# Score matmuls of two attentions with queries stacked high over low, and a reordered attention stage

## The chip, the cores and the metric

The kernel runs on one core of one Trainium2 chip. The metric is the device time in microseconds of one execution. The engines that matter are TensorE (PE; its weight loads are shown apart as PEld), VectorE (DVE), ScalarE (ACT), GpSimd (POOL) and SyncE (SP), which issues most of the DMAs.

## The reference

A trunk of two layers over 256 tokens of width 1024, in float32. Each layer is a feed-forward, a block of three attentions side by side, another feed-forward, and a gated projection. What matters here is the block of attentions (A, B, C below):

```python
n = rms_norm(h, norm_g[i, 1])
(aq, ak, av, bq, bkc, bvc, bks, bvs, bkw, bvw, bgate, cq, ck, cv, ga, gb, gc) = split_cols(n @ w_in[i], IN_SPLITS)
ya = diff_attention(...)       # A: 4 heads, two 64-wide maps each
yb = nsa_attention(...)        # B: 8 heads, 2 key groups; compressed, selected and window keys
yc = swa_sink_attention(...)   # C: 8 heads, 2 key groups, window 128, a sink
merged = (sigmoid(ga) * (ya @ w_branch[i, 0]) + sigmoid(gb) * (yb @ w_branch[i, 1])
          + sigmoid(gc) * (yc @ w_branch[i, 2]))
h = h + merged @ w_out[i]
...
s = jnp.einsum('bqgrd,bkgd->bgrqk', qi, kb, preferred_element_type=jnp.float32) * scale   # scores, d = 64
```

All heads are 64 wide. The scores of B's selected and window keys and of C are products of queries with keys over those 64 elements, then a bias is added and a softmax taken.

## The kernel before, in words

**Products in three parts.** Every float32 operand is split into a high part (rounded to the matmul's type) and a low part (the rest). A product is three matmuls into the same PSUM bank: high by high, high by low, low by high (`mul3`). Tokens lie in two tiles of 128 (`t`), the contraction in chunks of 128 (`k`).

**Main line and side work.** The program is one list of steps. `product` walks the chunks of one weight matrix for both token tiles; its weights come in 512 KB pieces through SP's queue, and each is split by ScalarE (`wh`) and VectorE (`wl`). After each chunk `product` calls `flow.tick()`. The attentions themselves (scores, softmax, transposes, value products) are generators handed to `Flow`; each tick adds the generator's pace (`PACE_A`, `PACE_B`, `PACE_C`) to a counter, and each whole unit runs it on by one `yield`. `flow.join` runs it to its end. So the paces and the order of the main line's products decide between which matmuls side work is written. A scheduler then orders the instructions of each engine by its own estimate; it may interleave the matmuls of different tiles, but those into one PSUM bank keep their order.

**The main line in attention:** A0, A1, A2 (queries, keys, values of A), then A's side work starts; Ck, Cq, Bk; C starts; Bv, Bq; gate and branch products of A (`ga0 ma0 ga1 ma1` in the new table's names); `second_weights`; B starts; `compress` (the `cmp` products of the compressed keys); gate and branch products of C; those of B, and the output projection.

**Scores.** `scores` (line 942) makes the scores of two head pairs `m`, each with two heads `par`. The high and low query parts lie in `q[:, 0]` and `q[:, 1]`; head `par` has its 64 elements in rows 64*par to 64*par+63. So each matmul uses 64 rows, and each head of the pair writes a PSUM bank of its own (`ps[par]`, tile name `s`). A call is 3 parts x 2 pairs x 2 heads = 12 matmuls. B has 6 calls a layer, C has 4, and A has 4. The keys stand twice in the partitions, once for each half (`done_ck`, `done_bk` copy them), so that both heads find theirs.

**Queries.** `done_q` scales a token tile of Cq or Bq, and `toT` transposes it on TensorE (tile `qt`) and splits it: one copy on ScalarE, one subtraction on VectorE, 128 partitions each.

**Compressed scores.** `compressed` lays the 16 compressed keys of a group block-diagonally (`kbd`), so that `attend_cmp` gets both heads of a pair from one `mul3` of 32 columns (tile `sc`): 12 matmuls a token tile.

Of the kernel before, what the change touches and what calls it, by code (L numbers as in the profile page):

```python
# [10 lines left out]
F32 = mybir.dt.float32  # L11
# [23 lines left out]
SPLIT = 16  # L35
TURNS = ('A0','A1')
ON_DVE = TURNS
# [7 lines left out]
POINTS = (5, 8, 11, 14, 18, 21)  # L45
PACE_A, PACE_B, PACE_C = 0.75, 0.72, 0.6

# [138 lines left out]
class Flow:  # L186
# [13 lines left out]

    def tick(self):
        for lane in self.lanes.values():
            if lane[0]:
                lane[1] += lane[0][0][1]
                while lane[1] >= 1.0 and lane[0]:
                    lane[1] -= 1.0
                    self.step(lane)
# [9 lines left out]
def trunk(ctx: ExitStack, tc: tile.TileContext, a: dict, out: bass.AP, index: list):  # L217
# [11 lines left out]
    def mm_bank(name):  # L229
        return bank("mm", 2, name)  # L230
# [169 lines left out]

    def product(lhs, nk, done, name, w, skew=SKEW):

        def run():
            ps = [None] * NT
            for step in range(nk + skew):
                for t, k in ((0, step), (1, step - skew)):
                    if 0 <= k < nk:
                        wh, wl = w(k)
                        if k == 0:
                            ps[t] = product_bank(f"{name}{t}")  # L410
                        xh, xl = lhs(t, k)
                        mul3(ps[t][:, :w.width], xh, xl, wh, wl, k == 0, k == nk - 1)
                        if k == nk - 1:
                            with tc.high_priority(offset=150):
                                done(t, ps[t])
                        flow.tick()
        return run
# [471 lines left out]
    def attention(i, norm, after):  # L889
# [41 lines left out]
        def scores(name, q, qb, t, key):  # L931
# [11 lines left out]
            return ps  # L943

        def softmax(p, ps, bias, sink=None):

            n = len(ps)
            st = pool.tile([128, 32], F32, tag="st", bufs=4, name="st")
            for j in range(n):
                low = 3.0e38 if sink is None else sink[:, j:j + 1]  # L950
                nc.vector.tensor_tensor_reduce(out=p[j], in0=ps[j], in1=bias[j], scale=-1.0, scalar=low,  # L951
                                               op0=ALU.add, op1=ALU.min, accum_out=st[:, j:j + 1])
                nc.scalar.activation(p[j], p[j], AF.Exp, bias=st[:, j:j + 1], scale=-1.0, accum_out=st[:, n + j:n + j + 1])  # L953
                if j % 2:
                    yield st
            yield st
# [136 lines left out]
        def done_q(dst, name):  # L1093
            def done(t, ps):
                if t == 0:
                    dst[0] = heads(name)
                sb = stage()
                nc.scalar.activation(sb, ps, AF.Copy, scale=norm.eighth(t))
                late_T(name, dst[0], t, 4, sb)
            return done  # L1100
# [11 lines left out]

        def compress():
            pos = pool.tile([128, 2, 2, 8], F32, name="pos")
# [3 lines left out]
            for kv in range(2):  # L1118
                for s in range(2):
# [3 lines left out]
                        pos[:, kv, s, :, None].to_broadcast([128, 8, 32 - s]), op=ALU.add)  # L1123
            es = base.tile([128, 2, 2, 8, 2, 32], F32R, tag="blk", bufs=6, name="es")
            ev = es.rearrange("p a b c x n -> p (a b c) x n")
            split(ev[:, :, 0], ev[:, :, 1], e.rearrange("p a b c n -> p (a b c) n"))
            c_ps = mm_bank("cmp")
            for kv in range(2):
                for k in range(16):
                    both = es[:, kv, k // 8, k % 8].rearrange("p x n -> p (x n)")  # L1130
                    wh, wl = w1(16 * kv + k)
                    o = c_ps[:64, kv * 256:(kv + 1) * 256]
                    nc.tensor.matmul(o, both, wh, start=k == 0, stop=False)
                    nc.tensor.matmul(o, both, wl, start=False, stop=k == 15)
                    flow.tick()
            c_sb[0] = pool.tile([128, 512], F32, name="c_sb")
            nc.vector.tensor_copy(c_sb[0][:64], c_ps[:64])

        def compressed():
# [21 lines left out]
            for f in range(2):  # L1161
                s, n = slice(128 * f, 128 * f + 128), slice(32 * f, 32 * f + 32)
                mul3(k_ps[:, :32], w2h[:, s], w2l[:, s], hid[:, 0, n], hid[:, 1, n], f == 0, f == 1)
            kbd = pool.tile([128, 2, 32], F32, name="kbd")
            nc.gpsimd.memset(kbd, 0.0)
            kv_ = k_ps[:, :32].rearrange("p (g n) -> p g n", g=2)
            nc.vector.tensor_copy(kbd[0:64, :, 0:16], kv_[0:64])
            nc.vector.tensor_copy(kbd[64:128, :, 16:32], kv_[64:128])
            kt = pool.tile([128, 2, 2, 32], F32R, name="kc")
            split(kt[:, 0], kt[:, 1], kbd)  # L1170
            yield
# [37 lines left out]
        def attend_cmp(t):  # L1209
            s_ps = tp_bank("sc")  # L1210
            for j in range(4):
                mul3(s_ps[:, 32 * j:32 * j + 32], qB[0][:, 0, j, t * 128:(t + 1) * 128], qB[0][:, 1, j, t * 128:(t + 1) * 128],
                     kc[0][:, 0, j // 2], kc[0][:, 1, j // 2], True, True)
            yield
            p = pool.tile([128, 8, 16], F32, tag="pc", bufs=2, name="pc")
            st = pool.tile([128, 32], F32, tag="st", bufs=4, name="st")
            nc.vector.tensor_tensor(p, s_ps[:, :128].rearrange("p (h n) -> p h n", h=8), cbias[:, t], op=ALU.add)
            nc.vector.tensor_reduce(st[:, 0:8], p, axis=AX.X, op=ALU.max)
# [26 lines left out]
        def attend_b():  # L1245
            bnd, y_ps = {}, {}

            def first(u):
# [3 lines left out]
                if t == 0:  # L1252
                    p = pool.tile([128, 4, 2, 128], F32, tag="p", bufs=3, name="p")
                    s = scores("s", qB[0], [2 * g, 2 * g + 1], 0, lambda x, r, m: kB[0][r, x, g:g + 3:2, :128])
                    rows = [(j, k) for j in range(4) for k in range(2)]
                    pr = [p[:, j, k] for j, k in rows]
                    sr = [s[j // 2].rearrange("p m (k n) -> p m k n", k=2)[:, j % 2, k] for j, k in rows]
                    br = [back(bnd[g][:, j], 128) for j, k in rows]
                else:
                    p = pool.tile([128, 4, 256], F32, tag="p", bufs=3, name="p")  # L1260
                    s = scores("s", qB[0], [2 * g, 2 * g + 1], 1, lambda x, r, m: kB[0][r, x, 2 * ss[0] + g, :])
                    pr = [p[:, j] for j in range(4)]
                    sr = [s[j // 2][:, j % 2] for j in range(4)]
                    br = [back(bnd[g][:, j], 256) for j in range(4)]
# [47 lines left out]
        def done_ck(t, ps):  # L1312
            if t == 0:
                kC[0] = heads("kC")
                vC[0] = pool.tile([128, NT, 2, 128], F32R, name="vC")
# [8 lines left out]
        def attend_c():  # L1324
# [4 lines left out]
            def first(u):  # L1329
                g, t = u  # L1330
                nk = 128 * (t + 1)
                if g not in bnd:
                    bnd[g] = band(12 + 4 * g)
                s = scores("s", qC[0], [2 * g, 2 * g + 1], t, lambda x, r, m: kC[0][r, x, g, :nk])
                yield
# [30 lines left out]
        def branch(b, yT, side, last=False):  # L1366
# [28 lines left out]
            def mixed(c, done):  # L1395
                return product(lambda t, k: (yT[t][:, 0, k, :], yT[t][:, 1, k, :]), 4, done, "br", streamed(i, f"br{b}{c}", 512), 4)

            both = [parts(c) for c in range(2)]
            if last:
                yield gated(0, both[0][0])  # L1400
# [31 lines left out]
                yield lambda: tile(1)  # L1432
            else:
                for c in range(2):
                    yield gated(c, both[c][0])
                    if c == 0:
                        yield lambda: flow.join(sides[side])
                    yield mixed(c, both[c][1])

        mT = [None] * NT  # L1440

        def project(name, done, width=512):
            return product(norm.lhs, NK, done, name, streamed(i, name, width))

# [6 lines left out]
        def start(name, side, pace, lane=0):  # L1451
            sides[name] = flow.start(side, pace, lane)

        yield turned_all
        yield lambda: start("a", attend_a(), PACE_A)
        yield project("Ck", done_ck, 256)
        yield project("Cq", done_q(qC, "qC"))
        yield project("Bk", done_bk)
        yield turned_all
        yield lambda: start("c", attend_c(), PACE_C)  # L1460
        wbv = a["wbv"][i]
        yield product(norm.lhs, NK, done_bv, "Bv",
                      Weights(280, [(wbv[:, k * 280:(k + n) * 280], n * 280) for k, n in ((0, 3), (3, 3), (6, 2))], 3))
        yield project("Bq", done_q(qB, "qB"))
        yield from branch(0, yA, "a")
        yield second_weights
        yield turned_all
        yield lambda: start("b", attend_b(), PACE_B)
        w1 = streamed(i, "w1", 256)
        yield compress  # L1470
        yield lambda: start("compressed", compressed(), 1.0, 1)
        yield from branch(2, yC, "c")
        yield from branch(1, yB, "b", True)
# [213 lines left out]
```

## Time and profile before

| what | value |
|---|---|
| median of three runs | 1306.36 us (1306.11 to 1306.38) |
| profiled execution, whole time | 1308.18 us |
| its span, first to last instruction | 1306.4 us |
| mean granted TensorE clock | 0.996 |
| busy: PE, PEld, DVE, ACT | 1294.4, 1068.1, 1092.9, 923.6 us |
| attention of layer 1, of layer 2 | 188 to 453 us, 830 to 1094 us of the span |
| score matmuls (line 942) | 96 of A, 96 of C, 144 of B |

A row of the timeline gives the start, the length, the engine, the source line, the operation, the tile written and those read, and the shape: `64*128 64x256` is a matmul with 64 active rows and 128 columns of weights, over 256 moving columns. An `x12` merges equal instructions that follow each other. Lengths of matmuls contain their way through the array, and overlap; the distance from one start to the next is what a matmul costs the queue.

### The profile page before, as it was taken

To read this page: it belongs to the slowest core of one execution; us is meant where nothing else is said; L and a number is where in the kernel's file an instruction comes from. 1 tells how busy PE (TensorE), PEld (TensorE's weight loads), DVE (VectorE), ACT (ScalarE), POOL (GpSimd) and SP (SyncE) were. 2 spreads that over 40 slices of the span, in tenths; PEclk is the share of its full clock that TensorE was granted. 3 is DMA by queue.
4 is the path that set the end of the run, shared out by engine and by line. 5 is a ranking of instruction groups with operands and counts; after the bars stand their busy time and mean duration, and the time that the engine had idled before them with its cause. 6 is when DMAs were issued, how large, how long until landed. Compare 5 with 4: busy or idle time off the path is not lost.

```text
span 1306.4 us, 17953 instructions
## 1 busy us (share of the span) xinstructions
PE 1294.4 (99%) x6242; PEld 1068.1 (82%) x6242; DVE 1092.9 (84%) x1754; ACT 923.6 (71%) x1468; POOL 28.6 (2%) x46
## 2 busy tenths in 40 slices
PE   8999999999999999999999999999999999999997
PEld 6888888887888888888888888888878888888886
DVE  7868977768978799998799999777687888999975
ACT  6777667658858577876667876666696775877664
POOL 0000000000000000000000000000000000000000
PEclk8999999999999999999999999999999999999999
DMA  8779688355743568787666787864556535677772
GB/s 307 228 226 277 192 247 235 122 185 167 239 140 122 164 195 241 223 226 225 209 195 231 202 249 227 252 177 160 178 166 205 162 129 180 206 211 227 236 229 83
DMA packets 137180, 263.76 MB, mean 202 GB/s; under 512 B 71670, under 2 KB 77174, under 8 KB 137088
## 3 DMA queue, kind: packets, MB, share of 16 engines
q1 hardware_dynamic: 134128, 252.57, 63.2%
q0 software_dynamic: 2528, 9.47, 2.2%
q8 instruction: 49, 0.80, 0.2%
q10 hardware_dynamic: 432, 0.56, 0.1%
q14 instruction: 43, 0.35, 0.1%
HBM read 245.75 MB, written 1.08 MB: 189 GB/s over the span
## 4 chain that ended last, share of the span: by engine, by line
PE 98%; issue 0%; DMA 0%; DVE 0%; ACT 0%; SPq 0%; POOLq 0%; POOL 0%; DVEq 0%; ACTq 0%
PE ff L267 8%; PE ff L265 8%; PE ff L266 8%; PE fo L266 5%; PE fo L265 5%; PE fo L267 5%; PE p L265 4%; PE p L266 4%; PE p L267 4%; PE gate L265 3%; PE gate L267 3%; PE gate L266 3%; PE s L942 3%; PE A L266 2%; PE br L265 2%; PE A L265 2%
## 5 line engine op out<-in xcount | busy, mean ns | idle before, releaser
L253 DVE TENSOR_TENSOR wl<-raw,wh 128x1024 fp32r<-128x1024 f32 (+1 forms) x426 | 510.3, 1213 | 94.9 <-ACT wh L258 93.4
L258 ACT ACTIVATE wh<-raw 128x1024 fp32r<-128x1024 f32 (+1 forms) x426 | 441.6, 1048 | 153.3 <-DMA raw<-in_wst 55.2
L267 PE MATMUL ff<-wh,nT 128*128 128x512 f32 x480 | 187.8, 393 | 0.6 <-DVE nT L253 0.6
L266 PE MATMUL ff<-wl,nT 128*128 128x512 f32 x480 | 188.0, 393 | 0.2 <-DVE wl L253 0.2
L265 PE MATMUL ff<-wh,nT 128*128 128x512 f32 x480 | 179.2, 393 | 1.2 <-ACT nT L443 1.2
L267 PE MATMUL fo<-wh,gT 128*128 128x512 f32 x304 | 117.2, 390 | 0.0
L266 PE MATMUL fo<-wl,gT 128*128 128x512 f32 x304 | 115.8, 389 | 0.0
L265 PE MATMUL fo<-wh,gT 128*128 128x512 f32 x304 | 114.3, 390 | 0.0
L265 PEld LDWEIGHTS ff<-wh,nT 128*128 128x128 f32 x480 | 90.7, 189 | 21.4 <-ACT nT L443 1.9
L267 PEld LDWEIGHTS ff<-wh,nT 128*128 128x128 f32 x480 | 90.8, 189 | 19.7 <-DVE nT L253 0.9
L266 PEld LDWEIGHTS ff<-wl,nT 128*128 128x128 f32 x480 | 90.8, 189 | 19.5 <-DVE wl L253 0.8
L267 PE MATMUL gate<-wh,nT 128*128 128x512 f32 x192 | 76.6, 399 | 0.0
L265 PE MATMUL gate<-wh,nT 128*128 128x512 f32 x192 | 76.4, 400 | 0.0
L266 PE MATMUL gate<-wl,nT 128*128 128x512 f32 x192 | 75.9, 395 | 0.0
L267 PEld LDWEIGHTS fo<-wh,gT 128*128 128x128 f32 x304 | 57.1, 188 | 11.8
L266 PEld LDWEIGHTS fo<-wl,gT 128*128 128x128 f32 x304 | 57.1, 188 | 11.7
L265 PEld LDWEIGHTS fo<-wh,gT 128*128 128x128 f32 x304 | 57.1, 188 | 11.7
L953 ACT ACTIVATE p<-p,st 128x128 f32<-128x128 f32 (+1 forms) x128 | 56.7, 448 | 5.3 <-DVE st L951 5.0
L567 ACT ACTIVATE whole<-flip 128x1024 uint16<-128x1024 uint16 x32 | 43.0, 1364 | 20.8 <-DMA flip<-cut 20.7
L561 ACT ACTIVATE cut<-gated 128x1024 uint16<-128x1024 uint16 (+1 forms) x48 | 46.3, 974 | 9.3 <-DVE gated L601 9.3
L253 DVE TENSOR_TENSOR wl<-x,wh 128x1024 fp32r<-128x1024 f32 x42 | 50.5, 1222 | 2.0 <-ACT wh L258 2.0
L258 ACT ACTIVATE wh<-x 128x1024 fp32r<-128x1024 f32 x42 | 43.8, 1049 | 5.2 <-DVE x L253 4.0
(389 smaller groups left out, 2752.6 us busy)
## 6 DMA issues: line engine op xcount, KB each, us to landing
raw<-in_wst SPq DMA_DIRECT2D x424, 512.0 KB, 4.4
y<-in_wst POOLq DMA_DIRECT2D x6, 1024.0 KB, 6.6
band<-table SPq DMA_DIRECT2D x10, 512.0 KB, 5.0
xy<-in_wst POOLq DMA_DIRECT2D x4, 512.0 KB, 4.1
raw<-in_wbv SPq DMA_DIRECT2D x4, 420.0 KB, 3.2
xt<-in_xt SPq DMA_DIRECT2D x4, 256.0 KB, 5.6
raw<-in_wst SPq DMA_DIRECT2D x4, 256.0 KB, 5.2
h<-in_x SPq DMA_DIRECT2D x2, 512.0 KB, 7.5
```

What stands on the lines that cost most here:

```text
L253: nc.vector.tensor_tensor(o, x, y, op=ALU.subtract)
L258: nc.scalar.activation(hi, src, AF.Copy)
L265: nc.tensor.matmul(ps, xh, wh, start=start, stop=False, **kw)
L266: nc.tensor.matmul(ps, xh, wl, start=False, stop=False, **kw)
L267: nc.tensor.matmul(ps, xl, wh, start=False, stop=stop, **kw)
L561: nc.scalar.activation(cut.rearrange("p (w n) -> p w n", w=2), halves(src)[:, :128 * m].rearrange("p n w -> p w n"), AF.Copy)
L567: tc.keep_in_program_order(nc.vector.tensor_copy(to, of) if late else nc.scalar.activation(to, of, AF.Copy))
L942: nc.tensor.matmul(o, q[r, x, qb[m], t * 128:(t + 1) * 128], kk, start=x + y == 0, stop=x == 1)
L953: nc.scalar.activation(p[j], p[j], AF.Exp, bias=st[:, j:j + 1], scale=-1.0, accum_out=st[:, n + j:n + j + 1])
```

## The change

Three things are done at once.

1. **Stacked queries.** For B and C, `done_q` writes a query tile with the high part of head `par` in that head's 64 rows and its low part in the other 64. With the keys standing twice, one matmul over all 128 rows gives high by high plus low by high. A second, over the head's own 64 rows, gives high by low. `stacked` replaces `scores` in B and C: 8 matmuls a call, of which 4 use 128 rows and 4 use 64. The compressed scores take two matmuls of 32 columns a head (key high and key low beside each other) without the block-diagonal tile, and one more addition on VectorE.
2. **Order.** The main line follows the table `ORDER`: Bv moves ahead of Bk, C's side work starts before Bv, and B's starts after `ga1`, ahead of `cmp`, with `ma1` behind `cmp`. The preparation of the compression's tokens becomes a step of its own (`tokens`, `e` in the table).
3. **Weights by product.** `flow.tick(room)` multiplies the pace by a weight from `ROOM`, which depends on the product; the three paces change.

```diff
+ROOM = {'A0': 1, 'A1': 1, 'A2': 1, 'Ck': 0.5, 'Cq': 1.0, 'Bk': 1.0, 'Bv': 0.547, 'Bq': 1.5, 'cmp': 0.35, 'br0': 1.0, 'br2': 1.0}
+ORDER = 'Ck Cq C! Bv Bk Bq ga0 ma0 ga1 e B! cmp ma1 gc0 mc0 gc1 mc1'
...
-PACE_A, PACE_B, PACE_C = 0.75, 0.72, 0.6
+PACE_A, PACE_B, PACE_C = 0.931, 0.76, 0.69
...
-    def tick(self):
+    def tick(self, work=1.0):
         for lane in self.lanes.values():
             if lane[0]:
-                lane[1] += lane[0][0][1]
+                lane[1] += lane[0][0][1] * work
...
+        def stacked(name, q, qb, t, key):
+
+            ps = [psum.tile([128, 2, 256], F32, tag="s", bufs=2, name=name) for _ in range(2)]
+            for m in range(2):
+                for y in range(2):
+                    for par in range(2):
+                        r = slice(64 * par, 64 * par + 64) if y else slice(0, 128)
+                        kk = key(y, r, m)
+                        o = ps[par][:, m, :math.prod(kk.shape[1:])]
+                        if len(kk.shape) == 3:
+                            o = o.rearrange("p (s n) -> p s n", s=kk.shape[1])
+                        nc.tensor.matmul(o, q[r, par, qb[m], t * 128:(t + 1) * 128], kk, start=y == 0, stop=y == 1)
+            return ps
...
-                late_T(name, dst[0], t, 4, sb)
+                ps = tp_bank("qt")
+                transposes(ps, [sb[:, 128 * k:128 * k + 128] for k in range(4)])
+                v, ts = ps.rearrange("p (k q) -> p k q", q=128), slice(t * 128, (t + 1) * 128)
+                rows = [slice(0, 64), slice(64, 128)]
+                for par in range(2):
+                    nc.scalar.activation(dst[0][rows[par], par, :, ts], v[rows[par]], AF.Copy)
+                for par in range(2):
+                    sub(dst[0][rows[1 - par], par, :, ts], v[rows[par]], dst[0][rows[par], par, :, ts].bitcast(F32))
...
-            kbd = pool.tile([128, 2, 32], F32, name="kbd")
-            nc.gpsimd.memset(kbd, 0.0)
-            kv_ = k_ps[:, :32].rearrange("p (g n) -> p g n", g=2)
-            nc.vector.tensor_copy(kbd[0:64, :, 0:16], kv_[0:64])
-            nc.vector.tensor_copy(kbd[64:128, :, 16:32], kv_[64:128])
-            kt = pool.tile([128, 2, 2, 32], F32R, name="kc")
-            split(kt[:, 0], kt[:, 1], kbd)
+            kt = pool.tile([128, 2, 2, 16], F32R, name="kc")
+            split(kt[:, :, 0], kt[:, :, 1], k_ps[:, :32].rearrange("p (g n) -> p g n", g=2))
...
-                mul3(s_ps[:, 32 * j:32 * j + 32], qB[0][:, 0, j, t * 128:(t + 1) * 128], qB[0][:, 1, j, t * 128:(t + 1) * 128],
-                     kc[0][:, 0, j // 2], kc[0][:, 1, j // 2], True, True)
+                for par in range(2):
+                    o = slice(64 * j + 32 * par, 64 * j + 32 * par + 32)
+                    nc.tensor.matmul(s_ps[:, o], qB[0][:, par, j, t * 128:(t + 1) * 128],
+                                     kc[0][:, j // 2].rearrange("p x n -> p (x n)"), start=True, stop=True)
...
-                s = scores("s", qC[0], [2 * g, 2 * g + 1], t, lambda x, r, m: kC[0][r, x, g, :nk])
+                s = stacked("s", qC[0], [2 * g, 2 * g + 1], t, lambda x, r, m: kC[0][r, x, g, :nk])
```

How the instructions stand is shown at three places. The names in the rows are the tile written and the tiles read, with buffer numbers; `x6` merges equal rows.

First, TensorE at C's scores for the first key group and the second token tile. The two `s` tiles are the banks of the two heads. Before:

```order
L267 MATMUL br0_2917<-wh_2829,yA_2153 128x512
L942 MATMUL s_2624<-kC_2031,qC_2203 128x256 x3
L942 MATMUL s_2625<-kC_2031,qC_2203 128x256 x3
L942 MATMUL s_2624<-kC_2031,qC_2203 128x256
L942 MATMUL s_2625<-kC_2031,qC_2203 128x256
...
L273 MATMUL yt_2521<-ident_66,yn_2508 128x128
```

and now:

```order
L267 MATMUL gate1_2882<-wh_2805,nT_1529 128x512
L958 MATMUL s_2636<-kC_2025,qC_2170 128x256 x3
L958 MATMUL s_2637<-kC_2025,qC_2170 128x256 x3
L958 MATMUL s_2636<-kC_2025,qC_2170 128x256
L958 MATMUL s_2637<-kC_2025,qC_2170 128x256
L268 MATMUL gate1_2882<-wl_2806,nT_1529 128x512
```

Before, the pair of single rows comes three times, and all twelve matmuls have 64 rows. Now there are eight, and within a bank they are in turn of 128 and of 64 rows, so the row `x3` is 128, 64, 128. The call now stands in A's second gate product, where it stood in A's first branch product.

Second, TensorE at B's scores for the second token tile (first group). Before:

```order
L1134 MATMUL cmp_3149<-wl_3312,es_3146 64x256
L265 MATMUL gate0_3382<-wh_3345,nT_1443 128x512
L942 MATMUL s_3578<-kB_2364,qB_2687 128x256 x6
L942 MATMUL s_3579<-kB_2364,qB_2687 128x256 x6
L266 MATMUL gate0_3382<-wl_3346,nT_1443 128x512
```

and now:

```order
L1160 MATMUL cmp_3101<-wh_3203,es_3098 64x256
L958 MATMUL s_3519<-kB_2497,qB_2691 128x256 x4
L267 MATMUL br0_3276<-wh_3217,yA_2193 128x512
L1161 MATMUL cmp_3101<-wl_3204,es_3098 64x256
...
L958 MATMUL s_3520<-kB_2497,qB_2691 128x256 x4
L268 MATMUL br0_3276<-wl_3218,yA_2193 128x512
```

The call was one unbroken run of 64-row matmuls behind `cmp`; now each bank's four (128, 64, 128, 64 rows) stand apart, among `cmp` and A's second branch product.

Third, ScalarE at C's queries. Before:

```order
L1098 ACTIVATE stage<-Cq_2217,stats 128x512
L258 ACTIVATE wh<-raw 128x840
L258 ACTIVATE qC<-qt 128x4x128
L261 ACTIVATE yA<-yt,small 128x256
L258 ACTIVATE pT<-pt 128x512
```

and now:

```order
L1114 ACTIVATE stage<-Cq_2104,stats 128x512
L260 ACTIVATE kC<-qt 128x2x128
L260 ACTIVATE pT<-pt 128x256
L260 ACTIVATE wh<-raw 128x560
L1120 ACTIVATE qC<-qt 64x4x128 x2
```

One copy of 128 partitions has become two of 64.

More of the change, by code (lines that the diff above doesn't have):

```diff
@@ L35 @@
 SPLIT = 16
-TURNS = ('A0','A1')
+ROOM = {'A0': 1, 'A1': 1, 'A2': 1, 'Ck': 0.5, 'Cq': 1.0, 'Bk': 1.0, 'Bv': 0.547, 'Bq': 1.5, 'cmp': 0.35, 'br0': 1.0, 'br2': 1.0}
+ORDER = 'Ck Cq C! Bv Bk Bq ga0 ma0 ga1 e B! cmp ma1 gc0 mc0 gc1 mc1'
+TURNS = ('A0', 'A1')
 ON_DVE = TURNS
@@ L399, in last_product, with product @@
         return run
-    def product(lhs, nk, done, name, w, skew=SKEW):
+    def product(lhs, nk, done, name, w, skew=SKEW, room=1.0):
         def run():
@@ L415, in run @@
                                 done(t, ps[t])
-                        flow.tick()
+                        flow.tick(room)
         return run
@@ L1111, in attention, with tokens @@
         kc, vc, c_sb = [None], [None], [None]
-        def compress():
+        es = [None]
+        def tokens():
             pos = pool.tile([128, 2, 2, 8], F32, name="pos")
@@ L1123, in compress @@
                         pos[:, kv, s, :, None].to_broadcast([128, 8, 32 - s]), op=ALU.add)
-            es = base.tile([128, 2, 2, 8, 2, 32], F32R, tag="blk", bufs=6, name="es")
-            ev = es.rearrange("p a b c x n -> p (a b c) x n")
+            es[0] = base.tile([128, 2, 2, 8, 2, 32], F32R, tag="blk", bufs=6, name="es")
+            ev = es[0].rearrange("p a b c x n -> p (a b c) x n")
             split(ev[:, :, 0], ev[:, :, 1], e.rearrange("p a b c n -> p (a b c) n"))
+        def compress():
             c_ps = mm_bank("cmp")
@@ L1129, in compress @@
                 for k in range(16):
-                    both = es[:, kv, k // 8, k % 8].rearrange("p x n -> p (x n)")
+                    both = es[0][:, kv, k // 8, k % 8].rearrange("p x n -> p (x n)")
                     wh, wl = w1(16 * kv + k)
@@ L1134, in compress @@
                     nc.tensor.matmul(o, both, wl, start=False, stop=k == 15)
-                    flow.tick()
-            c_sb[0] = pool.tile([128, 512], F32, name="c_sb")
+                    flow.tick(ROOM['cmp'])
+            c_sb[0] = stage("c_sb")
             nc.vector.tensor_copy(c_sb[0][:64], c_ps[:64])
@@ L1216, in attend_cmp @@
             st = pool.tile([128, 32], F32, tag="st", bufs=4, name="st")
-            nc.vector.tensor_tensor(p, s_ps[:, :128].rearrange("p (h n) -> p h n", h=8), cbias[:, t], op=ALU.add)
+            s_ = s_ps[:, :256].rearrange("p (h x n) -> p h x n", h=8, x=2)
+            nc.vector.tensor_tensor(p, s_[:, :, 0], cbias[:, t], op=ALU.add)
+            nc.vector.tensor_tensor(p, p, s_[:, :, 1], op=ALU.add)
             nc.vector.tensor_reduce(st[:, 0:8], p, axis=AX.X, op=ALU.max)
@@ L1253, in first @@
                     p = pool.tile([128, 4, 2, 128], F32, tag="p", bufs=3, name="p")
-                    s = scores("s", qB[0], [2 * g, 2 * g + 1], 0, lambda x, r, m: kB[0][r, x, g:g + 3:2, :128])
+                    s = stacked("s", qB[0], [2 * g, 2 * g + 1], 0, lambda x, r, m: kB[0][r, x, g:g + 3:2, :128])
                     rows = [(j, k) for j in range(4) for k in range(2)]
@@ L1260, in first @@
                     p = pool.tile([128, 4, 256], F32, tag="p", bufs=3, name="p")
-                    s = scores("s", qB[0], [2 * g, 2 * g + 1], 1, lambda x, r, m: kB[0][r, x, 2 * ss[0] + g, :])
+                    s = stacked("s", qB[0], [2 * g, 2 * g + 1], 1, lambda x, r, m: kB[0][r, x, 2 * ss[0] + g, :])
                     pr = [p[:, j] for j in range(4)]
@@ L1313, in done_ck @@
             if t == 0:
-                kC[0] = heads("kC")
+                kC[0] = pool.tile([128, 2, 2, SEQ], F32R, name="kC")
                 vC[0] = pool.tile([128, NT, 2, 128], F32R, name="vC")
@@ L1395, in mixed, with closing @@
             def mixed(c, done):
-                return product(lambda t, k: (yT[t][:, 0, k, :], yT[t][:, 1, k, :]), 4, done, "br", streamed(i, f"br{b}{c}", 512), 4)
+                return product(lambda t, k: (yT[t][:, 0, k, :], yT[t][:, 1, k, :]), 4, done, "br", streamed(i, f"br{b}{c}", 512), 4, ROOM[f"br{b}"])
             both = [parts(c) for c in range(2)]
-            if last:
+            def closing():
                 yield gated(0, both[0][0])
@@ L1432, in branch, with piece @@
                 yield lambda: tile(1)
[L1433 to L1438, printed above, removed]
+            def piece(kind, c):
+                if kind == "g":
+                    return gated(c, both[c][0])
+                step = mixed(c, both[c][1])
+                return lambda: (flow.join(sides[side]), step())
+            return closing() if last else piece
         mT = [None] * NT
         def project(name, done, width=512):
-            return product(norm.lhs, NK, done, name, streamed(i, name, width))
+            return product(norm.lhs, NK, done, name, streamed(i, name, width), room=ROOM[name])
         yield begin
@@ L1452, in start @@
             sides[name] = flow.start(side, pace, lane)
+        wbv = a["wbv"][i]
+        parts_of = {"a": branch(0, yA, "a"), "c": branch(2, yC, "c")}
         yield turned_all
         yield lambda: start("a", attend_a(), PACE_A)
[L1456 to L1472, printed above, removed]
+        for x in ORDER.split():
+            if x[0] in "gm" and x[1] in "ac":
+                yield parts_of[x[1]](x[0], int(x[2]))
+            elif x == "Ck":
+                yield project("Ck", done_ck, 256)
+            elif x == "Cq":
+                yield project("Cq", done_q(qC, "qC"))
+            elif x == "C!":
+                yield lambda: start("c", attend_c(), PACE_C)
+            elif x == "Bk":
+                yield project("Bk", done_bk)
+            elif x == "e":
+                yield second_weights
+                yield tokens
+            elif x == "Bv":
+                yield product(norm.lhs, NK, done_bv, "Bv",
+                              Weights(280, [(wbv[:, k * 280:(k + n) * 280], n * 280) for k, n in ((0, 3), (3, 3), (6, 2))], 3), room=ROOM["Bv"])
+            elif x == "Bq":
+                yield project("Bq", done_q(qB, "qB"))
+            elif x == "B!":
+                yield lambda: start("b", attend_b(), PACE_B)
+            elif x == "cmp":
+                w1 = streamed(i, "w1", 256)
+                yield compress
+                yield lambda: start("compressed", compressed(), 1.0, 1)
         yield from branch(1, yB, "b", True)
```

## The prediction

> **What bounds the kernel now.** I read the page's busy times and chain first, then who waited on TensorE, then the two attention stages as windows, and last the timeline row by row where the score matmuls stand.
>
> ```profile
> PE 1294.4 (99%) x6242; PEld 1068.1 (82%) x6242; DVE 1092.9 (84%) x1754; ACT 923.6 (71%) x1468; POOL 28.6 (2%) x46
> PE 98%; issue 0%; DMA 0%; DVE 0%; ACT 0%; SPq 0%; POOLq 0%; POOL 0%; DVEq 0%; ACTq 0%
> ```
>
> ```profile
> PE warm L1633 <- DVE idle L1628: 1.5, 1, 1.5
> ```
>
> ```profile
> 188.10:452.80 264.70, 264.70 (x1424) 218.19 (x1423) 206.32 (x458) 183.46 (x391) 4.39 (x6) 1.00 0.56 174
> ```
>
> TensorE runs 99% of the span and the chain is TensorE for 98%. The row of the waits is the longest of its four, all of them in the opening, on tiles of the first products (`warm`, `ff`). The window (columns: length, then PE, PEld, DVE, ACT, POOL busy, granted clock, DMA share, GB/s) is the first layer's attention stage; the second's, 830 to 1094, reads the same. There the clock is full, PE has no gap, VectorE 206 of 265 us, ScalarE 183, the DMA engines half. So no reordering can win back a wait here, for there is none; the change is worth what it takes from, or adds to, the time TensorE needs to go through its own queue. I measure that from start to start, since ends are modelled.
>
> **What a score matmul costs.** The next rows are a run of twelve score matmuls of the first attention, in which the two PSUM banks alternate, and six of the second attention that all write one bank.
>
> ```profile
> 228.42 0.28 PE L266 MATMUL Ck<-wl,nT 128*128 128x256 f32 x1
> 228.63 0.98 PE L942 MATMUL s<-qkA 64*128 64x256 f32 x12
> 229.54 0.39 PE L267 MATMUL Ck<-wh,nT 128*128 128x256 f32 x1
> 229.76 0.28 PE L265 MATMUL Ck<-wh,nT 128*128 128x256 f32 x1
> ```
>
> ```profile
> 332.86 0.28 PE L1134 MATMUL cmp<-wl,es 128*64 128x256 f32 x1
> 333.07 0.98 PE L942 MATMUL s<-kB,qB 64*128 64x256 f32 x6
> 333.98 0.33 PE L1133 MATMUL cmp<-wh,es 128*64 128x256 f32 x1
> ```
>
> Twelve that alternate take 0.91 us (228.63 to 229.54); six of one bank alone take the same 0.91 (333.07 to 333.98). A bank belongs to one half of the 128 rows (64*128 in the row), so a matmul on the lower half runs beside one on the upper half for nothing. "Three products" of a head pair cost three slots for two heads. The stacked form has two 128-row products, one per head, and two 64-row ones: three slots again if the 64-row ones stand together, four if not. The matmul count falls by a third; the slots do not.
>
> **What a visit to 64-row matmuls costs.** Here one, then three, of them stand between full-height matmuls.
>
> ```profile
> 318.68 0.39 PE L267 MATMUL gate<-wh,nT 128*128 128x512 f32 x1
> 319.00 0.38 PE L942 MATMUL s<-kB,qB 64*128 64x256 f32 x1
> 319.31 0.50 PE L1194 MATMUL yc<-pT,vC 128*128 128x512 f32 x1
> 319.65 0.40 PE L1193 MATMUL yc<-pT,vC 128*128 128x512 f32 x1
> 319.88 0.39 PE L265 MATMUL br<-wh,yA 128*128 128x512 f32 x1
> 320.11 0.39 PE L1194 MATMUL yc<-pT,vC 128*128 128x512 f32 x1
> ```
>
> ```profile
> 305.41 0.39 PE L267 MATMUL gate<-wh,nT 128*128 128x512 f32 x1
> 305.73 0.61 PE L942 MATMUL s<-kC,qC 64*128 64x256 f32 x3
> 306.27 0.50 PE L1193 MATMUL yc<-pT,vC 128*128 128x512 f32 x1
> 306.70 0.62 PE L942 MATMUL s<-kC,qC 64*128 64x256 f32 x3
> 307.25 0.50 PE L265 MATMUL gate<-wh,nT 128*128 128x512 f32 x1
> 307.59 0.40 PE L266 MATMUL gate<-wl,nT 128*128 128x512 f32 x1
> ```
>
> Undisturbed, a 512-column matmul follows the next after 0.23 us (319.88 to 320.11) and a 256-column one after about 0.115 (the cmp rows below show 0.11, the Ck rows' own stretch 0.12). From 318.68 to 319.88 stand three of 512 (0.68) and one of 256 (0.115), 0.80 in all; it took 1.20, so the visit cost 0.40. The second block holds three of 512 and six of 256, 1.37, and took 2.18: two visits, 0.40 each, though only one full-height matmul parts them. The long run at 228 took 1.34 (228.42 to 229.76) less two Ck (0.23) and six pairs (0.69): 0.42. So a visit costs 0.40 whether it is one matmul or twelve. For 128 columns:
>
> ```profile
> 215.22 0.40 PE L265 MATMUL A<-wh,nT 128*128 128x512 f32 x1
> 215.55 0.33 PE L942 MATMUL s<-qkA 64*128 64x128 f32 x2
> 215.80 0.50 PE L266 MATMUL A<-wl,nT 128*128 128x512 f32 x1
> 216.14 0.39 PE L267 MATMUL A<-wh,nT 128*128 128x512 f32 x1
> ```
>
> 0.92 less two of 0.23 and one slot of 0.11 is 0.36; handing on from a lone 128-column slot took 0.25 (215.55 to 215.80), 0.14 over its slot, so where both neighbours are that short I take 2 x 0.145 = 0.29, an estimate.
>
> [...]
>
> ```profile
> 338.52 0.28 PE L1133 MATMUL cmp<-wh,es 128*64 128x256 f32 x1
> 338.63 0.28 PE L1134 MATMUL cmp<-wl,es 128*64 128x256 f32 x1
> 338.74 0.40 PE L265 MATMUL gate<-wh,nT 128*128 128x512 f32 x1
> ```
>
> [...]
>
> **The sum.** What the second and third attention's scores cost now, 240 matmuls in 36 visits (18 a layer, counted as unbroken runs of such rows in the timeline):
>
> ```profile
> L942 PE MATMUL s<-kB,qB 64*128 64x256 f32 x144 | 16.9, 305 | 0.0
> L942 PE MATMUL s<-kC,qC 64*128 64x256 f32 x48 | 6.9, 303 | 0.0
> L942 PE MATMUL s<-kC,qC 64*128 64x128 f32 x48 | 4.1, 281 | 0.0
> ```
>
> From start to start, less what the neighbours would take without them, the 36 visits come to 32.2 us. The rows check it: 27.9 us busy, and behind each visit the first full matmul takes 0.34 for 0.23 (319.31 to 319.65, 307.25 to 307.59), 36 x 0.11 = 4.0, so 31.9.
>
> Afterwards there are 20 calls of eight matmuls. Within a bank they stand full, half, full, half, so a row "x4" of one bank is two visits. Counted over the whole order: 12 calls are full and half in strict turn, four visits (8 with 256 columns, 4 with 128); 6 run three visits, seven slots; 2 run two visits, six slots: 70 visits. Priced: 8 x (8 x 0.115 + 4 x 0.40 = 2.52) = 20.2; 4 x (8 x 0.11 + 4 x 0.29 = 2.04) = 8.2; 6 x (7 x 0.115 + 3 x 0.40 = 2.0) = 12.0; 2 x (6 x 0.115 + 0.80) = 3.0; together 43.4 us, 11.2 more than now. That a full-height score matmul of 256 columns costs 0.115 is the Ck and cmp spacing; the trace shows no full-height score, but its shape is theirs.
>
> The compressed scores go from 48 to 32 matmuls, each 0.11 us:
>
> ```profile
> 368.86 0.26 PE L267 MATMUL sc<-kc,qB 128*128 128x32 f32 x1
> 368.98 0.26 PE L265 MATMUL sc<-kc,qB 128*128 128x32 f32 x1
> ```
>
> 16 x 0.11 = 1.8 us less. The first attention's code is untouched, but in the new order its scores fall into 10 runs a layer, where it was 9: 2 x 0.40 = 0.8 more. Sum: 11.2 + 0.8 - 1.8 = +10.2 us.
>
> Off TensorE: each stacked query costs ScalarE two half-height copies instead of one and VectorE two subtractions. Their nearest rows are the present ones:
>
> ```profile
> L258 ACT ACTIVATE qC<-qt x4: 597/598/598, 246.4 to 894.7; 128x512 fp32r<-128x512 f32 x4
> L253 DVE TENSOR_TENSOR qC<-qt,qC x4: 684/688/692, 247.2 to 895.4; 128x512 fp32r<-128x512 f32 x4
> ```
>
> Half the partitions take no less time if length along the row sets it: eight more of each with Bq's, 4.8 us on ScalarE and 5.5 on VectorE in two layers; a few short copies of the block-diagonal key go and four short additions come. VectorE has 58 us of room a layer, so I cost this at nothing. If that cover were gone it would show as softmax late for the transposes. The reordered products, the weights by product and the new paces cost nothing by themselves: with no wait on TensorE they only choose where side work lands, and what that does to visits is counted above. The w2 and pos loads move on SP's queue ahead of w1, and w1 ahead of the first branch's last two weight tiles; the bytes are the same and the DMA engines are at 0.56.
>
> From this execution's span, 1306.4, that is 1316.6. It ran 1308.2 in all with what lies around the span; the median of the three runs is 1306.36, and I add the 10.2 to that.
>
> **Bounds.** The cheapest hand-over that the rows show is cmp to score, 0.21 against 0.11 (332.86 to 333.07). Were both sides of every visit that cheap, 0.20 a visit: 13.8 + 6.7 + 8.4 + 2.2 = 31.1, so -1.1 + 0.4 - 1.8 = -2.5 us: 1303.9. At the dearest, 0.42 a visit (0.36 for 128 columns), 54 x 0.02 + 16 x 0.07 = 2.2 more: 1318.8. I take 0.40, since two places with one parting matmul gave just that.
>
> **Rivals.**
> 1. Matmul count decides (faster): if every matmul cost one weight load, 0.11 us, 96 fewer would be 96 x 0.11 = 10.6 us off, 1295.8. For it: PEld is busy 82%, and single-file scores go at about that step. Against it: twelve loads in 0.91 us at 228. [...] It decides only if pairs stopped running together. Chance 0.07.
> 2. The cheap hand-over (no change): 1304 to 1306. Against it, the 0.40 came out three times. Chance 0.07.
> 3. A new wait on top (slower still): while cmp runs, the other engines are full.
>
> ```profile
> 327.50:338.70 11.20, 11.20 (x85) 9.94 (x84) 11.12 (x43) 10.96 (x34) 0.00 (x0) 1.00 0.63 200
> ```
>
> ```profile
> L253 DVE TENSOR_TENSOR wl<-raw,wh 128x1024 fp32r<-128x1024 f32 (+1 forms) x426 | 510.3, 1213 | 94.9 <-ACT wh L258 93.4
> ```
>
> VectorE 11.12 and ScalarE 10.96 of 11.20 (the first row, the stretch of cmp). The w1 splits there feed cmp; the new order starts the second attention ahead of cmp and puts three of its score calls beside it. If VectorE falls behind by a split (1.2 us in the second row) and a softmax bank, TensorE waits about 2 us a layer: 1320 to 1322. For it is the full window, against it that TensorE did not wait with the same fullness. Chance 0.08.
>
> **Numbers.** My forecast, visits at 0.3 to 0.42, has 0.78: 1311 to 1319, centre 1316.5. A measurement here tells 0.2% (2.6 us) from nothing. Faster by more: rival 1 and the lower edge of 2, 0.10. Within: the rest of 2 and a cheap end of the forecast, 0.08. Slower: 0.82. The range 1308 to 1321 leaves out rivals 1 and 2 and the top of 3.
>
> **What would show it.** Right: TensorE still without waits in attention, its score rows broken into full and half ones, steps of about 0.31 us between a full and a half score of 256 columns, attention stages about 5 us longer each, the feed-forward stages unchanged, q copies of about 0.6 us. Wrong: steps of 0.21 or less at these places, full-height score matmuls that start within a few ns of a half one, or waits of TensorE for softmax banks or w1 splits.

## The result, and the profile after

The changed kernel takes 1317.95 us (median of four runs, 1317.44 to 1318.31); the kernel before, on the same chip, 1306.37 (1306.11 to 1306.92). The ratio is 1.0083, interval 1.0071 to 1.0095: slower by 11.6 us. The profiled execution took 1317.44 us with a span of 1315.6.

First, of the page after, the busy times and the chain; then the longest waits of TensorE (engine, line, what it waited for: total us, times, longest).

```profile
PE 1303.0 (99%) x6146; PEld 1070.8 (81%) x6146; DVE 1098.4 (83%) x1762; ACT 932.2 (71%) x1476; POOL 26.4 (2%) x44
PE 98%; DVE 1%; issue 0%; DMA 0%; ACT 0%; SPq 0%; POOLq 0%; POOL 0%; DVEq 0%; ACTq 0%
```

```profile
PE warm L1671 <- DVE idle L1666: 1.5, 1, 1.5
PE ff L267 <- ACT nT L445: 1.0, 1, 1.0
PE mt L275 <- DVE pT L255: 0.8, 2, 0.4
```

TensorE runs 96 matmuls fewer and is busy 8.6 us longer; it is still the whole chain. In attention one wait is new, `mt`, once a layer. Then the stages as windows (columns as before): both attentions, from the first `A` matmul to the first of the next feed-forward; then what lies between them and behind them, of the kernel after and of the kernel before.

```profile
186.70:456.70 270.00, 269.61 (x1375) 220.18 (x1374) 209.46 (x463) 188.06 (x396) 4.27 (x6) 1.00 0.55 171
833.70:1104.00 270.30, 269.92 (x1379) 220.58 (x1378) 209.79 (x463) 188.37 (x396) 4.27 (x6) 1.00 0.55 170
```

```profile
456.75:833.74 376.99, 376.99 (x1682) 312.13 (x1681) 344.25 (x410) 276.77 (x336) 7.25 (x12) 1.00 0.73 221
1104.04:1315.60 211.56, 202.79 (x927) 168.74 (x925) 182.49 (x230) 146.94 (x188) 5.33 (x9) 0.99 0.67 203
```

```profile
452.80:829.80 377.00, 377.00 (x1682) 312.27 (x1681) 344.31 (x410) 276.86 (x336) 8.31 (x13) 1.00 0.73 220
1094.80:1306.40 211.60, 203.01 (x927) 168.70 (x925) 182.47 (x230) 146.58 (x188) 6.23 (x9) 0.99 0.67 202
```

Attention is 264.7 and 265.0 us before, 270.0 and 270.3 after: 5.3 more in each layer, 10.6 in all. Everything else is the same to 0.1 us but the opening (186.7 after, 188.1 before), where the profiled execution of before ran 6.8 us at the half clock (0.50 granted in 10 to 14 us, 0.83 over the first 20) and that of after 3.4 (0.50 in 10 to 12 us, 0.91 over the first 20). That is most of why the two spans differ by 9.2 us and the medians by 11.6.

Where the 5.3 us are is seen in the timeline after. Three stacked calls follow: C with 128 columns, C with 256, and one bank of B among `cmp` and C's value products. A row takes full and half matmuls of one tile together and prints the first one's shape.

```profile
259.37 2.01 PE L958 MATMUL s<-kC,qC 128*128 128x128 f32 x8
261.31 0.50 PE L267 MATMUL Bk<-wh,nT 128*128 128x512 f32 x1
261.65 0.40 PE L268 MATMUL Bk<-wl,nT 128*128 128x512 f32 x1
```

```profile
290.34 1.96 PE L958 MATMUL s<-kC,qC 128*128 128x256 f32 x8
292.22 0.50 PE L268 MATMUL gate<-wl,nT 128*128 128x512 f32 x1
```

```profile
330.17 1.22 PE L958 MATMUL s<-kB,qB 128*128 128x256 f32 x4
331.32 0.50 PE L1215 MATMUL yc<-pT,vC 128*128 128x512 f32 x1
331.66 0.39 PE L1216 MATMUL yc<-pT,vC 128*128 128x512 f32 x1
```

The first call takes 1.94 us to the next start, and the matmul behind it 0.11 more than its 0.23. Eight slots of 0.11 are 0.88, so four visits cost (1.94 + 0.11 - 0.88) / 4 = 0.29 each. The second takes 1.88, and the matmul behind it 0.12 more than usual; it holds three visits and seven slots of 0.115, so a visit costs (1.88 + 0.12 - 0.805) / 3 = 0.40. The bank of B: 1.49 from 330.17 to 331.66, less one of 0.23 and four of 0.115, is 0.80: two visits, 0.40 each. Over both layers the stacked scores cost 43.1 us from start to start (32.2 before), A's scores 13.2 (12.4 before), the compressed scores 3.8 (5.4 before). One more kind of matmul has 64 rows, `gl`, the first product behind `cmp`: its eight matmuls a layer stood in two visits and now stand in one, 2.4 us for 2.9.

Two readings of the other engines close the view: the query copies on ScalarE and VectorE, and the window of `cmp`.

```profile
L1120 ACT ACTIVATE qC<-qt x8: 579/592/594, 239.8 to 896.7; 64x512 fp32r<-64x512 f32 x8
L255 DVE TENSOR_TENSOR qC<-qt,qC x8: 683/689/694, 241.0 to 898.1; 64x512 fp32r<-64x512 f32 x8
```

```profile
322.00:337.00 15.00, 15.00 (x98) 12.34 (x97) 14.20 (x50) 14.50 (x44) 0.00 (x0) 1.00 0.69 212
```

Half the partitions take the whole time (592 and 689 ns for 598 and 688), and beside `cmp` VectorE and ScalarE are at 14.20 and 14.50 of 15.00 us with no gap on TensorE.

### The profile page after: what moved, and what is told of

Read it like the earlier page. It is cut to its first block, busy times and chain, and to the rows that moved or that the text cites. A ratio compares the mean times of both kernels' runs of the same rounds, so it can differ in the third digit from the quotient of the medians.

```text
span 1315.6 us, 17753 instructions
## 1 busy us (share of the span) xinstructions
PE 1303.0 (99%) x6146; PEld 1070.8 (81%) x6146; DVE 1098.4 (83%) x1762; ACT 932.2 (71%) x1476; POOL 26.4 (2%) x44
## 3 DMA queue, kind: packets, MB, share of 16 engines
HBM read 245.75 MB, written 1.08 MB: 188 GB/s over the span
## 4 chain that ended last, share of the span: by engine, by line
PE 98%; DVE 1%; issue 0%; DMA 0%; ACT 0%; SPq 0%; POOLq 0%; POOL 0%; DVEq 0%; ACTq 0%
PE ff L269 8%; PE ff L268 8%; PE ff L267 8%; PE fo L269 5%; PE fo L267 5%; PE fo L268 5%; PE p L267 4%; PE p L268 4%; PE p L269 4%; PE gate L268 3%; PE gate L269 3%; PE gate L267 3%; PE s L958 3%; PE br L267 2%; PE br L268 2%; PE A L268 2%
## 5 line engine op out<-in xcount | busy, mean ns | idle before, releaser
L255 DVE TENSOR_TENSOR wl<-raw,wh 128x1024 fp32r<-128x1024 f32 (+2 forms) x426 | 510.4, 1212 | 99.1 <-ACT wh L260 96.0
L260 ACT ACTIVATE wh<-raw 128x1024 fp32r<-128x1024 f32 (+2 forms) x426 | 442.4, 1048 | 166.3 <-DMA raw<-in_wst 60.8
L267 PEld LDWEIGHTS ff<-wh,nT 128*128 128x128 f32 x480 | 90.5, 189 | 20.9 <-ACT nT L445 1.7
```

The lines of the kernel that those rows point to most:

```text
L255: nc.vector.tensor_tensor(o, x, y, op=ALU.subtract)
L260: nc.scalar.activation(hi, src, AF.Copy)
L267: nc.tensor.matmul(ps, xh, wh, start=start, stop=False, **kw)
```

## The experiments

In the expectations V is the theory of visits (the time is what handing over between 64-row and full-height matmuls costs), O that the order and the paces did it, C that the count of matmuls decides. The kernel before ran beside all of them, at 1306.7 to 1306.8 us (1306.37 beside the changed kernel). Visits are those of the scores, counted in the executed order: 54 before (36 of B and C, 18 of A), 90 after. The visits of `gl` come on top: four in the kernel before, two in every other version but that of the price alone, which has four.

**All matmuls of a stacked call full-height.** The second product then adds low by low, which the reference's product contains; count, order and paces stay. 20 visits remain, A's.

```diff
-                        r = slice(64 * par, 64 * par + 64) if y else slice(0, 128)
+                        r = slice(0, 128)
```

> The changed kernel with one line different: the second score matmul of a stacked call also takes all 128 rows, so it adds low by low as well. Same 8 matmuls a call, same order table, paces and weights; no 64-row matmul is left in B and C (20 visits to 64-row matmuls, all of A, where the changed kernel has 90). Theory V (a visit costs 0.40 us, scores cost their slots): B's and C's scores fall from 43.1 us (measured in the changed kernel from start to start) to 16 x 0.92 + 4 x 0.88 = 18.2, so 1318.0 - 24.9 = 1293, clearly faster than the kernel before too. Theory O (the new order, paces and weights cost the time): no change, about 1318. Theory C (each matmul costs a fixed price): no change, for the count is the same. Between 1300 and 1312 would mean both V and something else.

Measured: 1297.65 us (1296.76 to 1298.9), ratio 0.9933 (0.9919 to 0.9946). One slice is worth 20.3 us against the changed kernel, at the same number of matmuls: O and C fall. Against V's number 4.6 us are missing. The timeline beside `cmp` shows calls of four full scores and then where TensorE waits; below it the wait of that tile and the window around it.

```profile
324.33 0.64 PE L958 MATMUL s<-kB,qB 128*128 128x256 f32 x4
324.81 0.40 PE L1215 MATMUL yc<-pT,vC 128*128 128x512 f32 x1
325.05 0.40 PE L1216 MATMUL yc<-pT,vC 128*128 128x512 f32 x1
325.65 0.33 PE L1161 MATMUL cmp<-wl,es 128*64 128x256 f32 x1 [0.20 <-DVE wl L255]
...
327.13 0.40 PE L267 MATMUL br<-wh,yA 128*128 128x512 f32 x1
328.05 0.34 PE L1161 MATMUL cmp<-wl,es 128*64 128x256 f32 x1 [0.52 <-DVE wl L255]
```

```profile
PE cmp L1161 <- DVE wl L255: 1.7, 4, 0.5
322.00:331.00 9.00, 8.23 (x58) 7.05 (x57) 8.96 (x29) 9.00 (x35) 0.00 (x0) 1.00 0.64 209
```

Four scores in 0.48 us, 0.12 each: no visit. But VectorE is now busy 8.96 of 9.00 us and ScalarE 9.00, and two steps that should take 0.23 take 0.60 and 0.92. So the work beside `cmp` needs its own time; in the changed kernel, whose scores take longer there, TensorE did not have to wait for it. In the two attention stages (259.4 and 260.0 us) 20.9 of V's 24.9 us are found. Of the 4.0 that are missing, the long steps at `cmp` hold 2.5, those around one `br` matmul a layer 0.6, and the scores with the matmul behind them some 0.8.

**The same, and A's scores kept together**, so that a call of A is not parted by other matmuls. 12 visits remain.

```diff
-                        nc.tensor.matmul(o, q[r, x, qb[m], t * 128:(t + 1) * 128], kk, start=x + y == 0, stop=x == 1)
+                        tc.keep_in_program_order(nc.tensor.matmul(o, q[r, x, qb[m], t * 128:(t + 1) * 128], kk, start=x + y == 0, stop=x == 1))
```

> All stacked score matmuls with 128 rows as in e1, and the first attention's twelve 64-row matmuls of a call kept in the order in which they are written, so that the two heads alternate. 12 visits to 64-row matmuls where e1 has 20, the same count of matmuls. Theory V: 8 x 0.40 = 3.2 us under e1's 1297.6, some 1294.5. If a visit's price were hidden under the waits that e1 has around cmp: about 1297.6.

Measured: 1294.62 us (1293.82 to 1295.32), ratio 0.9906 (0.9892 to 0.9919): 3.0 us for 8 visits, 0.38 each, a rougher figure than the others, since the executions of either version spread over 1.5 to 2.1 us. This is the fastest version of the study; it beats both kernels.

**The price of a visit alone.** In the kernel before, 120 high-by-high matmuls of the feed-forward (chunks 2 and 5) use only the lower 64 rows, which leaves out half of their sum. 103 visits more, the same count, order and paces.

```diff
+                        r = slice(0, 64) if k in (2, 5) else slice(0, 128)
+                        nc.tensor.matmul(ps[t], xh[r], wh[r], start=k == 0, stop=False)
```

> The price of a visit, away from attention: in the kernel before, 120 of the feed-forwards' 512-column matmuls (high by high of the chunks 2 and 5 of the plain products) use only the lower 64 rows, which leaves out half of their sum. Count of matmuls, columns and slots as before; 103 more visits by the built order. Theory V: 103 x 0.40 = 41 us, 1347 (1340 to 1352). If a visit is free away from attention, 1306.

Measured: 1349.16 us (1349.0 to 1349.33), ratio 1.0325 (1.0306 to 1.0344). 42.5 us over 103 visits is 0.41 each. One of them in the timeline:

```profile
61.33 0.39 PE L656 MATMUL ff<-wh,nT 128*128 128x512 f32 x1
61.65 0.50 PE L654 MATMUL ff<-wh,nT 64*128 64x512 f32 x1
62.08 0.50 PE L655 MATMUL ff<-wl,nT 128*128 128x512 f32 x1
62.41 0.39 PE L656 MATMUL ff<-wh,nT 128*128 128x512 f32 x1
```

Steps of 0.32, 0.43 and 0.33 where 0.23 is usual: 1.08 less three of 0.227 is 0.40, and no wait is marked.

**Order, weights and paces alone**, with the scores, queries and compressed keys of before. 62 visits.

> The order alone: the new order, paces and weights with the old scores, queries and block-diagonal compressed keys. 62 visits by the built order, 8 more than before. Theory V: 8 x 0.40 = 3.2 us, 1309 to 1311. Theory O: the whole loss, 1316 to 1319.

```diff
-                    s = stacked("s", qB[0], [2 * g, 2 * g + 1], 0, lambda x, r, m: kB[0][r, x, g:g + 3:2, :128])
+                    s = scores("s", qB[0], [2 * g, 2 * g + 1], 0, lambda x, r, m: kB[0][r, x, g:g + 3:2, :128])
...
```

Measured: 1311.56 us (1310.77 to 1312.46), ratio 1.0037 (1.0024 to 1.005), at the upper edge of V and far from O. The stages are 266.9 and 267.2 us, with no wait of TensorE in them. Of the 4.9 us (3.1 to 6.5 by the interval), 8 visits at 0.40 make 3.2. Most of the rest is in the scores too: only 58 matmuls of B and C run beside one on the other half of the rows, where 76 did. From start to start B's and C's scores take 36.0 us (32.2 before) and A's 13.2 (12.4), together 4.6 more.

**Stacking alone**, with the old order, the old paces and all weights 1. 86 visits.

```diff
-ORDER = 'Ck Cq C! Bv Bk Bq ga0 ma0 ga1 e B! cmp ma1 gc0 mc0 gc1 mc1'
+ORDER = 'Ck Cq Bk C! Bv Bq ga0 ma0 ga1 ma1 e B! cmp gc0 mc0 gc1 mc1'
...
-PACE_A, PACE_B, PACE_C = 0.931, 0.76, 0.69
+PACE_A, PACE_B, PACE_C = 0.75, 0.72, 0.6
```

> Stacking alone: the changed kernel with the old order of products, the old paces and all weights 1. 86 visits to 64-row matmuls by the built order, 54 before and 90 in the changed kernel. Theory V: 32 visits more than before, fewer compressed scores: +9 to +11, so 1315 to 1318. Theory O: the time of the kernel before or a little less, 1300 to 1307.

Measured: 1326.63 us (1325.71 to 1329.14), ratio 1.0155 (1.0141 to 1.0169), above both expectations. It has fewer visits than the changed kernel and is 8.7 us slower. The waits and the first attention stage say why:

```profile
PE br L267 <- ACT th L1400: 2.7, 2, 1.4
PE ya L269 <- DVE pT L255: 1.4, 2, 0.7
PE mt L275 <- DVE pT L255: 1.2, 2, 0.8
187.72:461.81 274.09, 270.30 (x1376) 219.77 (x1374) 209.24 (x462) 186.38 (x396) 4.69 (x6) 1.00 0.54 168
```

TensorE is idle 3.8 us of that stage (274.09 less 270.30), where it had no gap before. The second layer's stage is 275.2 us, so the two stages together are 9.0 us longer than in the changed kernel. ScalarE (`th`, in the gates) and VectorE (`pT`, the softmax's transposes) are late, though they are busy 0.68 and 0.76 of the stage only. The mean hides two cases. Around the `ya` wait of this stage (262 to 270 us) VectorE is busy 7.67 of 8.00 us. In front of the `br` wait ScalarE had room (10.80 of 15.00 us from 345 to 360); the chain of work that ended there shows what it stood for:

```profile
353.77 5.61 DMA raw<-in_wst
...
359.49 0.07 ACT wh L260
...
360.45 0.68 ACT th L1400
361.17 0.50 PE br L267
```

A weight piece was 5.61 us on its way; the split `wh` waited for it, and `th` came behind that split in ScalarE's order, with `br` behind `th`.

**Full height with the old order**: the slice of the first experiment together with the order and paces of the last. 18 visits.

> e1's full-height stacked scores with the old order of products, old paces and weights of 1 (18 visits). e2 (stacked in halves, same old order) took 1326.6, about 10 us over what its visits account for. Theory V with waits that belong to the old order with stacked queries: 68 visits fewer than e2, 27 us, 1299 to 1303, TensorE still waiting. If those waits came from the 64-row matmuls themselves: 1294 to 1296, without waits.

Measured: 1310.72 us (1308.64 to 1312.13), ratio 1.0028 (1.0017 to 1.0039), above the expectation with waits. The waits are the same ones, and `cmp` joins them:

```profile
PE cmp L1161 <- DVE wl L255: 3.2, 5, 1.4
PE br L267 <- ACT th L1400: 2.3, 2, 1.6
```

So the new order, weights and paces are worth 13.1 us to the full-height scores (1310.72 to 1297.65) and 8.7 to the stacked ones, and cost 4.9 where the scores are those of before.

**New order, old paces, weights 1.** 82 visits.

```diff
-ROOM = {'A0': 1, 'A1': 1, 'A2': 1, 'Ck': 0.5, 'Cq': 1.0, 'Bk': 1.0, 'Bv': 0.547, 'Bq': 1.5, 'cmp': 0.35, 'br0': 1.0, 'br2': 1.0}
+ROOM = {'A0': 1, 'A1': 1, 'A2': 1, 'Ck': 1, 'Cq': 1, 'Bk': 1, 'Bv': 1, 'Bq': 1, 'cmp': 1, 'br0': 1, 'br2': 1}
-PACE_A, PACE_B, PACE_C = 0.931, 0.76, 0.69
+PACE_A, PACE_B, PACE_C = 0.75, 0.72, 0.6
```

> The changed kernel with the old paces and all weights 1, in the new order of products (82 visits, the changed kernel has 90, e2 in the old order 86). If the order removed e2's waits: 1318 - 8 x 0.40 = 1314.8. If the paces and weights removed them: 1322 to 1326, with waits on TensorE as in e2.

Measured: 1331.74 us (1331.13 to 1332.02), ratio 1.0188 (1.0173 to 1.0204), slower than either expectation. The waits on `br` and `ya` are gone with the order; one new wait a layer has come, and what follows it is a surprise. Timeline, then windows; the column behind POOL's is the granted clock.

```profile
279.61 0.27 PE L269 MATMUL ya<-va,pT 128*128 128x128 f32 x1
281.47 5.52 PE L958 MATMUL s<-kC,qC 128*128 128x256 f32 x16 [1.58 <-DVE st L967]
...
294.79 0.63 PE L269 MATMUL gate<-wh,nT 128*128 128x512 f32 x1
295.22 0.63 PE L267 MATMUL gate<-wh,nT 128*128 128x512 f32 x1
```

```profile
266.00:279.60 13.60, 13.60 (x71) 11.54 (x71) 7.91 (x11) 7.41 (x14) 0.69 (x1) 1.00 0.61 197
282.00:298.00 16.00, 16.00 (x47) 11.61 (x47) 6.99 (x33) 11.03 (x41) 0.69 (x1) 0.57 0.26 90
298.00:315.00 17.00, 17.00 (x89) 13.93 (x89) 12.54 (x26) 13.55 (x29) 0.00 (x0) 1.00 0.32 104
937.00:953.50 16.50, 16.50 (x45) 11.52 (x45) 7.37 (x35) 11.11 (x41) 0.69 (x1) 0.50 0.25 92
```

TensorE waits 1.58 us for a softmax statistic, and then the clock is at the half (0.57 over the 16.00 us behind the wait in the first layer, 0.50 over 16.50 us in the second): gate matmuls step by 0.43 instead of 0.23. The lost clock is 16.00 x 0.43 = 6.9 us in the first layer and at least 16.50 x 0.50 = 8.2 in the second, some 15 together. Without it the time would be about 1316.6, an estimate, close to the changed kernel's. So the new order is free of the waits on `br` and `ya`, and the weights and paces remove this one.

**Each call grouped**: the four full-height matmuls first, then the four of 64 rows, kept in that order. 46 visits. The matmuls are the same, but the output is not: with a second pair's accumulation opened in a bank before the first pair's is closed, it is off by a relative error of 0.079.

```diff
-            for m in range(2):
-                for y in range(2):
+            for y in range(2):
+                for m in range(2):
...
```

> The changed kernel with a stacked call's four 128-row matmuls written first and its four 64-row ones last, kept in that order: 46 visits where the changed kernel has 90, the same matmuls and the same arithmetic. Theory V: 44 x 0.40 = 17.6 us, and the 64-row ones pair up (about 1 us more): 1318 - 18.6 = 1299.5, up to 1303 with e1's waits around cmp. Theory C or O: 1318.

Measured: 1304.82 us (1303.8 to 1307.5), ratio 0.9986 (0.9977 to 0.9994), above V's range and far below C and O. 44 visits fewer gave 13.1 us; by 0.40 they should have given 17.6. The rest stands mostly in new waits, 4.7 us together:

```profile
PE cmp L1161 <- DVE es L255: 2.1, 2, 1.0
PE gate L267 <- ACT yC L260: 1.5, 2, 0.8
PE gl L1172 <- DVE c_sb L1165: 1.1, 2, 0.5
```

## Why the prediction was right, and where it was not

The forecast was 1316.5 us, the measurement 1317.95.

- **Visits.** The price of 0.40 us carried the forecast and holds: 0.40 in two places of the trace after, 0.41 over 103 of them alone, 0.38 over eight taken away. The estimate for 128 columns was 0.29, and a whole call gave 0.29. The sum for B's and C's scores was 43.4 us; it is 43.1. Steps between full and half scores of 256 columns were said to be about 0.31, and 0.21 or less was to show the forecast wrong. From a half score to the next full matmul it is 0.31 every time. From a full score to a half one it is 0.31 only where the full one itself follows a half one (26 of 54); where it follows another full-height matmul (28 of 54) it is 0.21. So the sign was badly chosen: a visit of 0.40 is some 0.09 on the way in, 0.20 on the way out, and 0.11 on the first full matmul behind it.
- **The smaller terms.** A's extra run a layer was priced at 0.8 us and measured 0.8 (12.4 to 13.2). The compressed scores have 16 matmuls less; they were to save 1.8 us and saved 1.6. The two visits of `gl` that went, 0.5 us, were not in the sum. The stages close with these terms: 10.9 + 0.8 - 1.6 - 0.5, and 1.1 for the new wait below, is 10.7, and the stages grew by 10.6.
- **The feed-forward** was to be unchanged and is, to 0.1 us.
- **The q copies** were to take about 0.6 us and take 0.59 and 0.69. The cover was said to be ample. It held, but not for the reason given: 58 us of room a layer is a mean, and beside `cmp` there is little (14.20 of 15.00), none once the visits are gone (8.96 of 9.00).
- **No waits in attention** missed by one: `mt` waits for VectorE's split of a transposed softmax tile (`pT`) and steps 0.78 us for 0.23 once a layer, 1.1 us in all.

```profile
425.48 0.40 PE L1215 MATMUL yb<-pT,vB 128*128 128x512 f32 x1
426.26 0.66 PE L275 MATMUL mt<-ident,merged 128*128 128x128 f32 x4 [0.39 <-DVE pT L255]
```

- **The step that failed**, though the total came out, is that with no wait on TensorE the new order, weights and paces only choose where side work lands and have no wait to win back. With the old scores that holds as far as the runs tell: 4.9 us, no wait, nearly all of it in how the scores stand. With the new scores it does not: without the new order, weights and paces the kernel is 8.7 us slower with four visits less, and TensorE waits in its attention stages. The prediction took "no wait now" for "no wait after". The total came out because I counted visits over the changed order and that order happens to avoid the waits, which I had not asked of it; that part is luck.
- **Rivals.** The count (1295.8) is refuted by the full-height kernel: the same count, 20.3 us apart. The cheap hand-over (0.20 a visit) is refuted by the 0.41; the step of 0.21 that it was taken from is the way in alone. The new wait at `cmp` did not come in the changed kernel, but it comes as described, VectorE full and a split of w1 late, as soon as the scores are cheap.

What stays open: why the old order and paces bunch VectorE's work at `ya` and bring the weight piece late for `br`. One wait of each was followed back, in the first layer of the stacked kernel; those at `cmp` in the full-height kernel with the old order were not.

## What to carry to other kernels

Count a change of matmul shapes in slots and in hand-overs (here 0.115 us for a slot of 256 columns, 0.29 to 0.40 for a hand-over), not in matmuls: here a change with 96 matmuls less cost 11.6 us, mostly because it brought 34 more hand-overs between 64-row and full-height work (36 more of the scores, two fewer of `gl`). If half-height matmuls stand in strict turn with full ones, making them full-height, even with a product that is of no use, can be the cheaper form; it turned this change from a loss of 0.8% into a gain of 0.7%, and of 0.9% with A's scores kept together. When TensorE becomes faster in a stretch, look at the other engines of that same stretch, for the mean over the stage can hide that they are full there, or stand waiting for a weight piece: in the stacked kernel with the old order VectorE's 0.76 hid 7.67 of 8.00 us around `ya`, and ScalarE's 0.68 a piece that was 5.61 us on its way.

## What the runs showed that was not expected

A wait of TensorE of 1.58 us (1.86 from start to start) was followed by half the clock, about 13.8 us long in one layer (an estimate: 6.9 lost, twice over) and at least 16.5 in the other (0.50 granted), while TensorE was busy all through. In the stacked kernel with the old order, a wait of 1.32 us for `br` left the clock of its stage, the first layer's, at 1.00. In the full-height kernel with the old order the window around a wait for `ya` and one for `Bq`, 0.61 us each, shows a short dip:

```profile
262.00:276.00 14.00, 12.78 (x69) 11.05 (x68) 9.02 (x19) 5.70 (x15) 0.69 (x1) 0.88 0.63 201
```

14.00 x 0.12 = 1.7 us lost, or 3.4 us if the clock stood at the half. What keeps the clock down for so long while TensorE is busy was not tested; the work there is scores of full and half height in turn and transposes, and the clock came back 4 us into a run of full-height gate matmuls (from 293.8 us; steps of 0.43 us until 297.78, of 0.23 from 298.37).
